# Rotary embedding, one core: tile 3 loaded in one piece, tile 1's store timed by VectorE, tile 2's store on GpSimd's queue

## The chip, the core and the metric

One core of one Trainium2 chip. The metric is the device time of one execution in microseconds. Times below are medians of runs that are all fast; the core's span in the profile is some 1.9 us shorter than the device time. Every batch of runs also timed the kernel before on the same chip, and a ratio is the mean time of a kernel's fast runs over that of the kernel before, so it is not quite the ratio of the medians quoted.

## The reference

`x` is 16 x 512 x 16 x 64 in fp32 (33.55 MB), `cos` and `sin` are 512 x 32. The first half of the last dimension is rotated in quarters and the second half is passed through, so every byte of `x` is read once and written once.

```python
x1, x2 = x[..., :32], x[..., 32:]
first  = x1[..., :16] * cos[..., :16] - x1[..., 16:] * sin[..., :16]
second = x1[..., :16] * sin[..., :16] + x1[..., 16:] * cos[..., :16]
out = concatenate([first, second, x2], axis=-1)
```

## The kernel before

`x` is cut into four tiles of 128 partitions x 64 KB, which pass through a ring of three places in SBUF. VectorE rotates half a tile (8 of 16 rows of 4 KB per partition) with four instructions, in place. Tile 3 takes the place of tile 0, so its load waits for tile 0's store to land.

```python
ring = const_pool.tile([P, NS, K, H, D], fp32)        # NS = 3, K = 16
# load(t, lo, hi) and store(t, lo, hi): one DMA each on nc.sync, rows lo to hi of tile t
load(0)
load(1)
load(2, 0, KC)                                         # KC = 8
# ... cos and sin are loaded on nc.gpsimd and spread into `table` (cut)

def rotate(t, lo, hi):
    # x1, c, s, b_t: views of rows lo to hi (cut)
    nc.vector.tensor_mul(out=b_t, in0=x1, in1=s)
    nc.vector.tensor_mul(out=x1, in0=x1, in1=c)
    nc.vector.tensor_sub(...)                          # cut
    nc.vector.tensor_add(...)                          # cut

def turn(t):
    rotate(t, 0, KC)
    rotate(t, KC, K)
    return store(t)

turn(0)
load(2, KC, K)
near = load(3, 0, KL)                                  # KL = 14
load(3, KL, K)
tc.add_manual_dep(turn(1).ins, near.ins.name, ...)     # tile 1's store waits for `near`
turn(2)
turn(3)
```

## Time and profile before

| | before |
|---|---|
| device time, three runs | 161.51 us (161.4 to 161.61) |
| profiled execution: time, span | 162.1 us, 160.3 us |
| VectorE busy | 112.4 us, its last instruction ends at 130.6 us |
| 16 DMA engines busy with SP's and GpSimd's packets | 97.6% + 0.2% of the span |
| tile 1's store issued, landed | 98.96, 120.72 us |
| tile 3's store issued, landed | 130.6, 159.29 us |

The landing times are the last of the 16 semaphore updates of a DMA in the trace. DVE is VectorE, POOL is GpSimd, SP is SyncE; q1 is the DMA queue that SP fills, q0 that of GpSimd. Below, "row" of a transfer means what one partition of it holds (64 KB of a whole tile), which is one packet of a DMA engine; 16 engines share the 128 partitions, so a tile is 8 rows for each engine. The rows that KC, KL and KM count in the code are others: the 16 pieces of 4 KB in each partition. The profiled execution was a long one (162.1 us). The prediction shows the page, the stretches and SP's waits. The order of the arithmetic and the stores around the changed wait is in the timeline (start and length in us, engine, line, operation; "x3" merges three issues, the first of them at the start shown):

```profile
90.28 4.43 DVE L96 TENSOR_TENSOR b_t<-ring,table 128x4096 f32<-128x4096 f32 x1
94.75 4.42 DVE L97 TENSOR_TENSOR ring<-ring,table 128x4096 f32<-128x4096 f32 x1
98.96 31.98 SPq L58 DMA_DIRECT2D out_dram<-ring  x3
```

Tile 1's store goes out at 98.96, in the middle of tile 2's second half.

### The profile page before, as it was taken

The page shows a single profiled execution, that of the slowest core. Times are in us where ns is not written, and L with a number is a line of the kernel's source. Part 1 is how long each engine was busy: PE and PEld are TensorE (multiplying, and loading weights), DVE is VectorE, ACT ScalarE, POOL GpSimd, SP SyncE. Part 2 cuts the span into 40 slices and gives each one's busy share as a digit, 9 for nine tenths or more (in the row PEclk, how much of TensorE's full clock was granted, in tenths as well). Part 3 has the DMA queues.
Part 4 walks back from the last instruction along what each step waited for, and adds up shares of the span by engine and source line. Part 5 has one row for each costly group of instructions (what it writes and reads, how often), then busy time and mean ns, then how long its engine had stood idle before and what let it go on. Part 6 is the DMA issues. An engine that isn't in the chain of part 4 may idle for free.

```text
span 160.3 us, 113 instructions
## 1 busy us (share of the span) xinstructions
DVE 112.4 (70%) x43; POOL 1.4 (1%) x6
## 2 busy tenths in 40 slices
DVE  1000959999999999999999999999999950000000
POOL 3000000000000000000000000000000000000000
DMA  7969969699699996999999995996996996996990
GB/s 262 540 262 540 491 294 523 278 507 491 294 392 441 474 523 262 523 392 392 499 482 458 458 444 253 546 523 262 523 523 262 523 507 278 523 507 278 523 507 16
DMA packets 1504, 67.24 MB, mean 419 GB/s; under 512 B 192, under 2 KB 192, under 8 KB 224
## 3 DMA queue, kind: packets, MB, share of 16 engines
q1 hardware_dynamic: 1440, 67.11, 97.6%
q0 software_dynamic: 64, 0.13, 0.2%
HBM read 33.69 MB, written 33.55 MB: 419 GB/s over the span
## 4 chain that ended last, share of the span: by engine, by line
DVE 59%; DMA 14%; issue 7%; DVEq 1%
DVE b_t L96 22%; DVE ring L97 22%; DMA ring<-in_x_dram 14%; DVE ring L101 10%; DVE ring L98 4%; DVEq L148 1%; DVEq L96 0%
## 5 line engine op out<-in xcount | busy, mean ns | idle before, releaser
L96 DVE TENSOR_TENSOR b_t<-ring,table 128x4096 f32<-128x4096 f32 x8 | 35.5, 4432 | 2.1 <-DMA ring<-in_x_dram 1.9
L97 DVE TENSOR_TENSOR ring<-ring,table 128x4096 f32<-128x4096 f32 x8 | 35.4, 4424 | 0.3
L98 DVE TENSOR_TENSOR ring<-ring,b_t 128x2048 f32<-128x2048 f32 x8 | 18.3, 2287 | 0.3
L101 DVE TENSOR_TENSOR ring<-ring,b_t 128x2048 f32<-128x2048 f32 x8 | 18.2, 2280 | 0.0
L73 DVE LOAD_MASK_SELECT spun<-stage x1 | 0.0, 14 | 14.4 <-DMA stage<-in_sin_dram 14.4
L83 DVE COPY table<-packed 32x1024 f32<-32x1024 f32 x4 | 2.7, 684 | 0.1
L80 DVE COPY packed<-spun 32x512 f32<-32x512 f32 (+3 forms) x4 | 1.7, 416 | 0.1
L61 DVE MEMSET stage<- 128x512 f32 x1 | 0.5, 485 | 0.9 <-PEq L137 0.9
L73 DVE STREAM_SHUFFLE spun<-stage 128x512 f32<-128x512 f32 x1 | 0.7, 723 | 0.0
L63 POOL DMA_DIRECT2D stage<-in_cos_dram x1 | 0.6, 649 | 1.3 <-DVE stage L61 1.3
L64 POOL DMA_DIRECT2D stage<-in_sin_dram x1 | 0.5, 532 | 0.0
L137 POOL MEMSET const-float32-0.0<- 128x1 f32 x1 | 0.1, 93 | 0.2 <-issue 0.2
L137 POOL MEMSET const-bfloat16-1.0<- 128x1 bf16 x1 | 0.1, 95 | 0.0
L137 POOL MEMSET const-uint8-127<- 128x1 uint8 x1 | 0.1, 93 | 0.0
L137 POOL MEMSET const-float32-1.0<- 128x1 f32 x1 | 0.1, 92 | 0.0
## 6 DMA issues: line engine op xcount, KB each, us to landing
ring<-in_x_dram SPq DMA_DIRECT2D x2, 4096.0 KB, 41.4
ring<-in_x_dram SPq DMA_DIRECT2D x1, 7168.0 KB, 26.4
ring<-in_x_dram SPq DMA_DIRECT2D x1, 1024.0 KB, 28.5
stage<-in_cos_dram POOLq DMA_DIRECT2D x1, 64.0 KB, 9.0
stage<-in_sin_dram POOLq DMA_DIRECT2D x1, 64.0 KB, 13.4
out_dram<-ring SPq DMA_DIRECT2D x4, 25.6
ring<-in_x_dram SPq DMA_DIRECT2D x2, 32.0
```

What stands on the lines that cost most here:

```text
L61: nc.vector.memset(stage[:, :, :, 0:Q], 0.0)
L63: nc.gpsimd.dma_start(out=spread[:, 0, 0], in_=cosf)
L64: nc.gpsimd.dma_start(out=spread[:, 0, 1], in_=sinf)
L73: nc.vector.stream_shuffle(out=spun[:], in_=stage.rearrange("p t k j -> p (t k) j")[:, :, 0:Q], mask=[j % PQ * REP for j in range(PB)],)
L80: nc.vector.tensor_copy(out=packed[0:n], in_=spun[q * PB : q * PB + n])
L83: nc.vector.tensor_copy(out=table[r * PB : (r + 1) * PB].rearrange("p t k c j -> p (t k) c j"), in_=packed.unsqueeze(2).to_broadcast((PB, ...
L96: nc.vector.tensor_mul(out=b_t, in0=x1, in1=s)
L97: nc.vector.tensor_mul(out=x1, in0=x1, in1=c)
L98: nc.vector.tensor_sub(out=x1[:, :, :, 0:Q], in0=x1[:, :, :, 0:Q], in1=b_t[:, :, :, Q:HF])
L101: nc.vector.tensor_add(out=x1[:, :, :, Q:HF], in0=x1[:, :, :, Q:HF], in1=b_t[:, :, :, 0:Q])
L137: nc = _bacc.Bacc("TRN2", target_bir_lowering=False, num_devices=1)
L148: with _tile.TileContext(nc) as tc:
```

## The change

Tile 3 is loaded by one DMA, without the short extra load. Tile 1's store is still held back by an added dependency, but now until VectorE has finished the pieces 8 to 12 of tile 2 (up to KM = 13), and no longer until a load lands. Tile 2's store is issued by GpSimd on its own queue, so that it does not stand in line behind tile 1's.

```diff
--- before.py
+++ after.py
@@ -31,7 +31,7 @@
     R = H * D
     NS = 3
     KC = K // 2
-    KL = 14
+    KM = 13
 
     xf = x.rearrange("b s h d -> (b s h d)").rearrange("(t p f) -> t p f", t=T, p=P)
     of = out.rearrange("b s h d -> (b s h d)").rearrange("(t p f) -> t p f", t=T, p=P)
@@ -54,8 +54,8 @@
     def load(t, lo=0, hi=K):
         return nc.sync.dma_start(out=rows(t, lo, hi), in_=xf[t, :, lo * R : hi * R])
 
-    def store(t, lo=0, hi=K):
-        return nc.sync.dma_start(out=of[t, :, lo * R : hi * R], in_=rows(t, lo, hi))
+    def store(t, lo=0, hi=K, queue=nc.sync):
+        return queue.dma_start(out=of[t, :, lo * R : hi * R], in_=rows(t, lo, hi))
 
 
     nc.vector.memset(stage[:, :, :, 0:Q], 0.0)
@@ -98,28 +98,32 @@
         nc.vector.tensor_sub(
             out=x1[:, :, :, 0:Q], in0=x1[:, :, :, 0:Q], in1=b_t[:, :, :, Q:HF]
         )
-        nc.vector.tensor_add(
+        return nc.vector.tensor_add(
             out=x1[:, :, :, Q:HF], in0=x1[:, :, :, Q:HF], in1=b_t[:, :, :, 0:Q]
         )
 
-    def turn(t):
-        rotate(t, 0, KC)
-        rotate(t, KC, K)
-        return store(t)
-
-    turn(0)
+    rotate(0, 0, KC)
+    rotate(0, KC, K)
+    store(0)
     load(2, KC, K)
-    near = load(3, 0, KL)
-    load(3, KL, K)
+    load(3)
+    rotate(1, 0, KC)
+    rotate(1, KC, K)
+    behind_loads = store(1)
+    rotate(2, 0, KC)
+    near = rotate(2, KC, KM)
+    rotate(2, KM, K)
+    store(2, queue=nc.gpsimd)
 
     tc.add_manual_dep(
-        turn(1).ins,
+        behind_loads.ins,
         near.ins.name,
         mybir.DependencyInfo(mybir.DependencyClass.Sync, mybir.DependencyReason.DATA),
         reason="the store follows the loads at the DMA engines",
     )
-    turn(2)
-    turn(3)
+    rotate(3, 0, KC)
+    rotate(3, KC, K)
+    store(3)
 
 
 # ---- launch: one core; inputs and outputs as the reference has them ----
```

## The prediction

> **What bounds the kernel now.** I read the page first: its slices, its table of DMA queues, then its chain.
>
> ```profile
> span 160.3 us, 113 instructions
> DVE 112.4 (70%) x43; POOL 1.4 (1%) x6
> DMA packets 1504, 67.24 MB, mean 419 GB/s; under 512 B 192, under 2 KB 192, under 8 KB 224
> q1 hardware_dynamic: 1440, 67.11, 97.6%
> q0 software_dynamic: 64, 0.13, 0.2%
> ```
>
> VectorE (DVE) works 70% of the span and does nothing after its last instruction at 130.6 us. The 16 DMA engines are another matter: packets of the SP queue (q1) fill 97.6% of their time and those of GpSimd's queue (q0) 0.2%, together 97.8% of 160.3, or 156.8 us. Only 3.5 us are left, and the next view shows that they lie at the two ends. Its stretches are cut where a transfer ends in the trace's packet records, since packets of 64 KB would otherwise fall on either side of a cut; the columns are DVE busy, GpSimd busy, clock, DMA share and GB/s.
>
> ```profile
> 0.00:1.70 1.70, 0.48 (x1) 0.20 (x4) 1.00 0.00 0
> ...
> 22.10:52.10 30.00, 28.84 (x9) 0.00 (x0) 1.00 1.00 422
> 52.10:71.40 19.30, 19.16 (x6) 0.00 (x0) 1.00 0.99 431
> 71.40:100.50 29.10, 28.86 (x10) 0.00 (x0) 1.00 1.03 446
> 100.50:139.20 38.70, 29.87 (x10) 0.00 (x0) 1.00 1.01 439
> 139.20:158.40 19.20, 0.00 (x0) 0.00 (x0) 1.00 0.94 406
> 158.40:160.30 1.90, 0.00 (x0) 0.00 (x0) 1.00 0.00 0
> ```
>
> Nothing moves for 1.7 us at the start and 1.9 us at the end; between those the share is about 1.00 in every stretch (the 1.03 and 0.94 are packets counted whole on one side of a cut). So the kernel is bound by its transfers: 33.69 MB read and 33.55 MB written, on DMA engines that never pause. The packet records say the same more finely: a row of 64 KB takes 2.418 us on its engine, and its successor starts 2.41 to 2.42 us after it, also across the ends of transfers.
>
> Next, the waits of the SP queue, to see what orders the transfers.
>
> ```profile
> SPq L58 <- DVE ring L101: 57.7, 3, 26.9
> SPq L58 <- DMA ring<-in_x_dram: 46.5, 2, 25.6
> SPq L148 <- DMA out_dram<-ring: 28.3, 1, 28.3
> SPq L55 <- DMA out_dram<-ring: 21.7, 1, 21.7
> ```
>
> The 25.6 us is tile 1's store, ready when DVE finished tile 1 at 76.8 but held until the large part of tile 3's load landed at 98.9. It looks like a big cost, and it is the wait that the change rewrites. But the engines had loads to do in those 25.6 us, and the store's first packets start at 100.46, just where the short part of the load ends. A wait of the issuing queue costs time only if the DMA engines run dry, and here they don't. The chain of waits is of little use here: it follows DVE and stops at 130.6 us, though the last 28 us are stores alone.
>
> **What the Trainium skill says.** "DMA: Bandwidth & Descriptors", section "Issuing engines are not separate DMA queues", says that DMAs from SP, ScalarE and GpSimd end up on the same 16 engines and interleave, and that a second issuer saves only the time to issue. The trace agrees as far as it goes: an issue on SP takes 0.33 to 0.43 us, all of it beside transfers. The same page, "Queues, rings and completion order", says that an engine takes turns between the queues at packet granularity. The trace shows this in small: the 4 KB packets of cos and sin at 7.3 us go between two 64 KB packets without a gap. The section "SWDGE vs HWDGE vs iDMA" says that a packet of the software-made kind is preferably at most 4096 B. The cos and sin packets are 4096 B, but their rows are of 2 KB, so the trace does not tell what becomes of a 64 KB row. "SBUF — State Buffer", section "SBUF: two separate sides", warns that VectorE in a two-port mode locks GpSimd out while it writes descriptors. DVE's work here is tensor_tensor in fp32: 4.43 us for 4096 elements, or 1.08 ns each, so it runs at the plain rate and I do not expect that lock. No store from GpSimd in this trace shows it.
>
> **The change part by part.** Bytes do not change, nor do loads and stores in number of rows per engine: 64 rows of 64 KB each (67.11 MB over 16 engines and 65,536 B).
>
> *Load of tile 3 whole.* In the records a packet of 57,344 B takes 2.116 us, one of 8192 B 0.309. Each engine did 8 of each: 8 x (2.116 + 0.309) = 19.40 us. Now it does 8 x 2.418 = 19.34 us. That removes 0.06 us from the path that sets the end, and one semaphore packet of 0.009 us. Call it 0.07.
>
> *The wait of tile 1's store.* It now waits for the last instruction of rows 8 to 12 of tile 2. DVE starts the second half of tile 2 at 90.28. Its four kinds of instruction take 4.43, 4.42, 2.29 and 2.28 us for 8 rows. The split is about 1.04 ns an element and 0.15 us fixed, so for 5 of 8 rows: 2.83 + 2.82 + 1.49 + 1.48 = 8.62 us, less 0.08 overlap, plus gaps of 0.06. The store is released at about 98.9 us (estimate), where the load released it at 98.96. Load 3 should leave the earliest engines at about 100.4, and the first load took from 0.74 to 1.74 us between issue and first packet, so the store is in the ring just in time, as before. Gain nil; if the release came 0.3 us later, a gap of 0.3 us at most.
>
> *DVE.* Four instructions more, each for its fixed 0.15 us and a gap of 0.02: 0.7 us. DVE ends at 131.3 instead of 130.6. Tile 3's store then joins a queue that, in the before trace, is busy with tile 2's store until 139.1. So 8 us of slack absorb it.
>
> *Tile 2's store on GpSimd's queue.* Issued at about 104.5, it no longer stands behind tile 1's store but takes turns with it. What an engine has to do after 100.5 is 24 rows either way, 24 x 2.418 = 58.0 us, which is 100.4 to 158.4. Who goes first changes landing times, not the sum: the end follows tile 3's store or the remainder of tile 2's, whichever is last. The cost depends on packet size. With whole rows it is nil. Cut into 4 KB packets of 0.159 us (cos and sin rows), a row takes 16 x 0.159 = 2.544 us, and 8 rows 20.35 instead of 19.34: 1.0 us more, all of it on the path.
>
> The sum: -0.07 with whole rows, +0.94 with 4 KB packets. From 161.51 that makes 161.4 or 162.5 us.
>
> **The rivals.** *The early wait paid, and its removal gains.* For it: 25.6 us is the longest wait that touches this store. Against: the new wait ends at the same instant, and the DMA share beside it is full. Even with every gap and every slow packet gone (64 x 2.418 = 154.8 us of packets against 156.8 in the records) there are only 2.0 us to win, and those lie in the first 50 us, which the change does not touch: packets of tiles 0 and 1 took up to 3.3 us. So faster by 2%, 3.2 us, is nearly excluded.
>
> *GpSimd makes descriptors too slowly, and the engines starve.* If rows are cut to 4 KB, GpSimd must make 2048 pieces. Tile 1's store has then almost all the bandwidth until about 121, and tile 2's store alone feeds the engines from there until tile 3's store comes at 131. Against: the issues of cos and sin took 0.65 and 0.53 us for 32 rows, so at most 20 ns a row with the fixed part in it. At 20 ns, 2048 pieces take 41 us from 104.5. By 121 some 800 exist, by 132 some 1400, while engines at 4 KB per 0.159 us on each of 16 would use about 1100 in those 11 us. So no gap, or a small one. At twice that per piece the gap would be 3 to 4 us: 165 us, slower by 2%.
>
> *The mixture of two stores is slower than one.* The hardware queue's loads and stores ran at 2.418 us a row alike; nothing in the trace mixes two large transfers from two queues, so I can't exclude some per cent on 27 us of overlap. One per cent would be 0.3 us.
>
> **Range and chances.** I give whole rows 65%, 4 KB packets or another small cost of the second queue 30%, and starvation 5%. The middle lies near the first case, a little above: 161.6 us. The three runs of before span only 0.2 us, so the low end needs little room, 161.1; the high end takes in the 4 KB case, 162.7. Faster 1%, within 2% 96%, slower 3%.
>
> **What the profile of the changed kernel would show.** Packets of q0: 64 + 128 and their semaphores if rows stay whole, some 2100 if they are cut, with hundreds or thousands more in the page's count and the share of 16 engines' span up by about 0.6%. The DMA share should be full from 1.7 us to the end of the last store; tile 1's store issued between 98.7 and 99.2; DVE's end at 131.3; tile 1's store landing later than 120.7 if the two stores share evenly, near 121 if q0's packets are small. The prediction is wrong if the share drops below 0.95 anywhere between 100 and 158 us, if packets of 64 KB on q1 take clearly more than 2.418 us beside q0's, or if DVE's instructions after 104 us are longer than before.

## The result and the profile after

161.51 us (161.4 to 161.64, six runs) against 161.5 us (161.4 to 161.7, six runs): a ratio of 0.9999, 95% interval 0.9986 to 1.0012. The change does nothing to the time. The page's lines that answer to those of before:

```profile
span 159.5 us, 115 instructions
...
DVE 112.9 (71%) x47; POOL 1.9 (1%) x7
...
DMA packets 1360, 67.24 MB, mean 422 GB/s; under 512 B 176, under 2 KB 176, under 8 KB 208
...
q1 hardware_dynamic: 1152, 58.72, 85.7%
q0 software_dynamic: 208, 8.52, 12.4%
```

Tile 2's 8.39 MB have moved from q1 to q0. Of the 208 packets of q0, 32 are those of cos and sin, 48 are semaphore updates (three DMAs x 16 engines), which leaves 128: GpSimd's store kept its rows of 64 KB whole. Together the queues fill 98.1% of the span, against 97.8%. The stretches, cut at the ends of rows (DVE busy, GpSimd busy, clock, DMA share, GB/s):

```profile
22.00:51.00 29.00, 27.80 (x9) 0.00 (x0) 1.00 1.00 434
51.00:71.00 20.00, 19.86 (x6) 0.00 (x0) 1.00 1.02 434
71.00:99.80 28.80, 28.52 (x12) 0.00 (x0) 1.00 0.99 427
99.80:109.50 9.70, 9.56 (x6) 0.56 (x1) 1.00 1.00 432
109.50:131.20 21.70, 21.53 (x7) 0.00 (x0) 1.00 1.00 435
131.20:143.40 12.20, 0.00 (x0) 0.00 (x0) 1.00 0.99 430
143.40:157.90 14.50, 0.00 (x0) 0.00 (x0) 1.00 1.00 434
```

The DMA engines are as full as before. The page's span is 0.8 us shorter than that of before, but this is no gain: the unprofiled spans are 159.5 to 159.6 here and, in the later batches, 159.6 to 160.0 for the kernel before with one of 160.8, and the profiled execution of before had slow rows where nothing was changed (422 GB/s from 22.1 to 52.1 us, against 434 here). SP's waits and the timeline:

```profile
SPq L58 <- DVE ring L101: 84.1, 3, 30.5
...
SPq L58 <- DMA ring<-in_x_dram: 22.3, 2, 20.8
SPq L55 <- DMA out_dram<-ring: 21.0, 1, 21.0
```

```profile
97.35 1.48 DVE L101 TENSOR_TENSOR ring<-ring,b_t 128x1280 f32<-128x1280 f32 x1
98.86 32.68 SPq L58 DMA_DIRECT2D out_dram<-ring  x2
98.86 1.77 DVE L96 TENSOR_TENSOR b_t<-ring,table 128x1536 f32<-128x1536 f32 x1
...
104.31 4.43 DVE L96 TENSOR_TENSOR b_t<-ring,table 128x4096 f32<-128x4096 f32 x1
104.58 0.56 POOL L58 DMA_DIRECT2D out_dram<-ring  x1 [101.70 <-DVE ring L101]
```

The wait of 25.6 us for the load is gone, and one on VectorE has taken its place: tile 1's store goes out at 98.86 instead of 98.96. That is the same instant, 0.1 us apart. GpSimd's store goes out at 104.58, and the trace shows its rows from 109.52 on in strict turns with those of SP's queue, one of q0, one of q1, each 2.42 us, until the last row of tile 1's store ends at 129.2; then three rows of q0 follow each other, and the turns start again at 136.16 with tile 3's store. So tile 1's store lands at 132.05 instead of 120.72, tile 2's at 144.11 instead of 140.01, and the last at 158.58 instead of 159.29. The 24 rows per engine of the three last stores take 58.09 us on the earliest engine (99.85 to 157.94) and took 57.95 before (100.46 to 158.41): the sum is kept, the order is not.

### The profile page after: what moved, and what is told of

Read it like the earlier page. It is cut to its first block, busy times and chain, and to the rows that moved or that the text cites. A ratio compares the mean times of both kernels' runs of the same rounds, so it can differ in the third digit from the quotient of the medians.

```text
span 159.5 us, 115 instructions
## 1 busy us (share of the span) xinstructions
DVE 112.9 (71%) x47; POOL 1.9 (1%) x7
## 4 chain that ended last, share of the span: by engine, by line
DVE 61%; DMA 14%; issue 5%; DVEq 1%
DVE b_t L96 22%; DVE ring L97 22%; DMA ring<-in_x_dram 14%; DVE ring L101 10%; DVE ring L98 7%; DVEq L152 1%; DVEq L96 0%
## 5 line engine op out<-in xcount | busy, mean ns | idle before, releaser
L96 DVE TENSOR_TENSOR b_t<-ring,table 128x4096 f32<-128x4096 f32 (+2 forms) x9 | 35.6, 3959 | 2.1 <-DMA ring<-in_x_dram 1.9
L97 DVE TENSOR_TENSOR ring<-ring,table 128x4096 f32<-128x4096 f32 (+2 forms) x9 | 35.6, 3950 | 0.3
L98 DVE TENSOR_TENSOR ring<-ring,b_t 128x2048 f32<-128x2048 f32 (+2 forms) x9 | 18.4, 2050 | 0.3
L101 DVE TENSOR_TENSOR ring<-ring,b_t 128x2048 f32<-128x2048 f32 (+2 forms) x9 | 18.4, 2043 | 0.0
L58 POOL DMA_DIRECT2D out_dram<-ring x1 | 0.6, 559 | 101.7 <-DVE ring L101 101.7
```

Source lines behind the costliest of these rows:

```text
L58: return queue.dma_start(out=of[t, :, lo * R : hi * R], in_=rows(t, lo, hi))
L98: nc.vector.tensor_sub(out=x1[:, :, :, 0:Q], in0=x1[:, :, :, 0:Q], in1=b_t[:, :, :, Q:HF])
L101: return nc.vector.tensor_add(out=x1[:, :, :, Q:HF], in0=x1[:, :, :, Q:HF], in1=b_t[:, :, :, 0:Q])
```

## The experiments

First theory, the prediction's: the DMA engines are full, so queue and order don't matter and a wait costs only what time the engines stand dry. Rivals: two effects that cancel; a wait that does something although the engines are full; VectorE's chain as the bound.

### Tile 2's store back on SP's queue

```diff
-    store(2, queue=nc.gpsimd)
+    store(2)
```

> The changed kernel with tile 2's store back on SP's queue. Theory (the 16 DMA engines are full from 1.7 us on, so an issuer changes only who goes first): 161.4 to 161.6 us, as both kernels; tile 1's store lands near 120.5 instead of 132.05, tile 2's near 139.5 instead of 144.1, the last at 158.5 as before. In the mixed stretch of the changed kernel 24 rows per engine took 58.09 us against 57.95 in the kernel before, so at most 0.15 us is won back. Rival (two queues cost something that the whole load of tile 3 paid for, so that two effects cancel): 0.3 us or more faster than both.

161.77 us (161.52 to 161.83), ratio to the kernel before 1.0013 (1.0001 to 1.0025). Tile 1's store landed at 120.17, tile 2's at 139.47, the last at 158.78. The time is slightly above what was expected, and not below as the rival wants. From the landing of load 3 to the end this kernel took 158.78 - 100.88 = 57.90 us, the changed one 158.58 - 100.69 = 57.89. So GpSimd's queue neither costs nor gains. In the profiled executions the 0.2 us arose before 100 us, where the two programs are the same instruction for instruction: the rows that started from 67 to 75 us took 0.67 us too long per engine, against 0.38 in the changed kernel. I take it for a difference between chips or executions and have no run that shows which.

### The added wait taken out

```diff
-    tc.add_manual_dep(
-        behind_loads.ins,
-        near.ins.name,
-        ...
-    )
```

> The changed kernel with the added dependency of tile 1's store taken out (no data needs it), so that it is issued when VectorE has finished tile 1, near 76.8 us, behind tile 3's load on the same queue. Theory: the engines of a queue take rows in the order of issue, load 3 lands at 100.7 as before, time 161.4 to 161.6. Rival 1 (a store close behind a load disturbs it, which is what the wait was for): load 3 lands later than 102 or its rows take over 2.45 us, and the time rises by 1 us or more. Rival 2 (the wait held the kernel back): faster by 1 us or more.

162.87 us (162.56 to 162.9), ratio 1.008 (1.0068 to 1.0092): 1.4 us slower than the changed kernel's median. The first theory is wrong here, and rival 1 is right: the wait is worth more than a microsecond although no engine stands dry with it or without it. The store is issued at 76.84, and the place is visible in two stretches, first of the changed kernel, then of this one. The stretch 94.5 to 98.5 holds the start of exactly the last two rows of load 3 on each engine:

```profile
94.50:98.50 4.00, 3.97 (x3) 0.00 (x0) 1.00 1.21 524
```

```profile
94.50:98.50 4.00, 3.97 (x3) 0.00 (x0) 1.00 1.46 524
```

A packet is counted whole in the stretch in which it starts, so a share can exceed 1. The bytes are the same (524 GB/s), but the packets took 1.46 instead of 1.21 of the stretch: 0.25 x 4.0 = 1.0 us more on each engine. In the packet records it is the last row alone: 3.01 to 3.85 us, median 3.36, where the row before it and all store rows after it took 2.418. Everything after comes that much later: load 3 lands at 101.74 (100.69), the last store at 159.75 (158.58).

### Neither wait nor GpSimd's queue

```diff
-    store(2, queue=nc.gpsimd)
+    store(2)
-    tc.add_manual_dep(...)          # as in the run above
```

> The changed kernel with no added dependency and every store on SP's queue; load 3 stays whole. Theory: 161.4 to 161.6 us, so that neither kernel's arrangement does anything. If waits or queues each cost something that the other hides, this one differs from both by 0.3 us or more.

162.80 us (162.39 to 163.09), ratio 1.0078. It agrees with the run above within the spread: the cost belongs to the missing wait, on one queue or two. This kernel's profile is a poor witness: it is of its fastest execution (162.39), with the last row of load 3 at a median of 2.63 us, and 0.73 us per engine of its loss lie in slow rows between 20 and 47 us, as in the profile of the kernel before (0.78). So the cost at the last row is not the same in every execution.

### No arithmetic

```diff
-    rotate(0, 0, KC)
-    rotate(0, KC, K)
     ...                             # all rotations and the added wait out, transfers as they were
```

> The changed kernel's transfers without any rotation (a wrong result on purpose: the output is x); the added dependency goes with the arithmetic it hung on. Theory: nothing of VectorE's 107 us lies on the path that sets the end, so 161.3 to 161.6 us. Rival (the end is set by VectorE's chain at 131 us plus a last store, as the chain of waits suggests): many us faster.

162.71 us (162.19 to 163.25). Its output is wrong, which doesn't matter for the time. Without 107 us of VectorE's work the kernel is not faster, so VectorE's chain does not set the end. It is 1.2 us slower, which I had not expected. The trace points to the same cost at another place: with nothing to wait for, tile 0's store is issued at 22.98 instead of 49.87 and stands behind the loads of tile 1 and of tile 2's first half. The last two rows of 32 KB of tile 2's load before that store then took 1.87 and 1.69 us in the median (up to 2.14), where 1.213 is normal, 1.09 us more per engine; and here too the rows after the change of direction are normal:

```profile
47.50:52.30 4.80, 0.00 (x0) 0.00 (x0) 1.00 1.10 375
52.30:62.00 9.70, 0.00 (x0) 0.00 (x0) 1.00 1.03 446
```

A full share at 375 GB/s, then 446. In the other kernels VectorE releases tile 0's store at about 50 us, when the rows before it are nearly through. From 88 to 112 us this kernel also takes turns between load rows (q1) and store rows (q0); after one slower load row at the start of that (median 2.58), all took 2.418 but for single ones. So a change of direction between two queues does not cost each time.

### The point moved later

```diff
-    KM = 13
+    KM = 15
```

> The changed kernel with the point in tile 2's arithmetic moved two rows on (13 to 15): tile 1's store released near 102.1 instead of 98.86. Load 3's rows leave the engines from 99.85 to 100.26, and an issue took about 1.0 us to its first packet at the start, so the engines stand idle from about 100 to 103.1. Theory: a wait costs exactly the time for which the engines run dry: 3.0 to 3.4 us, 164.5 to 165.0 us. Rival (the wait's point doesn't matter, because tile 2's store or the slack at VectorE makes up for it): 161.5.

```diff
-    near = rotate(2, KC, KM)
-    rotate(2, KM, K)
+    rotate(2, KC, KM)
+    near = rotate(2, KM, K)
```

> The changed kernel with tile 1's store waiting for the end of tile 2's arithmetic, near 104.3 instead of 98.86; GpSimd's store is issued at the same time. Theory: engines idle from about 100.1 to 105.3, 5.0 to 5.4 us: 166.5 to 167.0 us, with a loss that is 2.2 us over that of the point at 15 rows, the further delay. Rival: 161.5, or a loss well under the delay.

164.72 us (164.28 to 164.85; ratio 1.0192) and 166.99 us (166.77 to 167.11; ratio 1.0336). Here the engines do stand dry, in the first and in the second kernel:

```profile
95.00:100.20 5.20, 5.17 (x3) 0.00 (x0) 1.00 0.93 403
100.20:103.00 2.80, 2.73 (x4) 0.00 (x0) 1.00 0.00 0
103.00:112.50 9.50, 9.40 (x5) 0.56 (x1) 1.00 1.03 442
```

```profile
95.00:100.20 5.20, 5.13 (x4) 0.00 (x0) 1.00 0.93 403
100.20:105.20 5.00, 4.90 (x5) 0.49 (x1) 1.00 0.00 0
105.20:115.00 9.80, 9.73 (x3) 0.07 (x1) 1.00 1.00 428
```

The stores go out at 102.24 and 104.44. Load 3's last rows end from about 99.95 to 100.4, the first store rows start at 103.08 and 105.29: some 3.0 and 5.2 us dry, against 3.2 and 5.5 us lost. The difference of the two, 2.3 us, is the 2.2 us between the issues. On this side the prediction's rule holds.

### The point moved earlier

```diff
-    KM = 13
+    KM = 11
```

> The changed kernel with the point moved two rows earlier (13 to 11), so that tile 1's store is released near 95.65, some 1.8 us before the last row of load 3 starts on the engines (97.43 to 97.84 in the changed kernel). The first theory (order alone counts) is already wrong by 1.3 us without the wait. Second theory: what costs is that a store stands in the queue when the last load row starts, however long it has stood there; then this costs as much as no wait, 162.5 to 163.0 us, with that row at 3.0 us or more in the trace. Rival: the cost grows with the time for which store and load are queued together; then most of it is gone, 161.5 to 161.9.

```diff
-    KM = 13
+    KM = 12
```

> The changed kernel with the point one row earlier (12): the store is released near 97.26, just before the last load row starts, and about 1.0 to 1.5 us later its rows can be fetched, so in the middle of that row. Second theory: the store comes after that row has started, so 161.4 to 161.7 us; rival (it must come after the row has nearly ended): 162.0 to 163.0.

162.66 us (162.47 to 162.91; ratio 1.006, 1.0038 to 1.0081) and 161.88 us (161.64 to 162.17; ratio 1.0017, 0.9993 to 1.0041). In one and the other, for the same two rows as above:

```profile
94.50:98.50 4.00, 3.93 (x4) 0.00 (x0) 1.00 1.47 524
```

```profile
94.50:98.50 4.00, 3.93 (x4) 0.00 (x0) 1.00 1.27 524
```

With the point two pieces earlier the store goes out at 95.57, 1.9 us before the last load row starts, and the whole cost is there: that row took 3.33 us in the median, as with a store that had stood in the queue since 76.84. With one piece earlier the store goes out at 97.24, as that row starts, and a part is left in the trace (2.67 us in the median, up to 3.00): 0.25 us per engine. Its median time is a little more than the second theory allowed, but the ratio's interval includes 1, so the time alone does not show this part. All six points together:

| tile 1's store issued | last row of load 3, median | engines dry | time |
|---|---|---|---|
| 76.84 (no wait) | 3.36 us | none | 162.87 us |
| 95.57 | 3.33 us | none | 162.66 us |
| 97.24 | 2.67 us | none | 161.88 us |
| 98.86 (the changed kernel) | 2.42 us | none | 161.51 us |
| 102.24 | 2.42 us | 3.0 us | 164.72 us |
| 104.44 | 2.42 us | 5.2 us | 166.99 us |

So the cost does not grow with the time the store stands in the queue; what counts, with these 64 KB rows, is whether it stands there when the last load row starts. The valley lies between 95.57 and 102.24, where the time has clearly risen on either side, and the changed kernel lies in it.

### The kernel before, without its wait

```diff
-    tc.add_manual_dep(
-        turn(1).ins,
-        near.ins.name,
-        ...
-    )
+    turn(1)
```

> The kernel before with its own wait taken out: tile 1's store is issued when VectorE has finished tile 1, near 76.8, instead of at 98.96. Second theory (a store that stands in the queue while the load's last rows start costs 1.0 to 1.3 us, and both kernels' waits avoid that to the same degree): 162.4 to 163.0 us, as the changed kernel without its wait. Rival (the short last load of 8 KB rows already protects the kernel before, and its wait is idle): 161.4 to 161.7.

162.65 us (162.23 to 162.95), ratio 1.0066 (1.005 to 1.0082). The old wait did the same work as the new one: without it the 8 KB packets of the short load took 0.4125 us in the mean instead of 0.3096, 0.8 us over the 8 packets of each engine. The first is this kernel, the second the kernel before:

```profile
97.80:100.60 2.80, 2.77 (x2) 0.00 (x0) 1.00 0.98 293
```

```profile
97.80:100.60 2.80, 2.77 (x2) 0.00 (x0) 1.00 1.43 609
```

(Fewer bytes start in the first stretch at a full share; the 1.43 is that of store rows which begin just before 100.6.) So the short load alone is no protection. Nor is it one packet alone that slows: the first 8 KB packet of each engine kept 0.310 us in the mean, the other seven took 0.427. With rows of 64 KB it was the last one, without arithmetic the last two of 32 KB, here seven of eight of 8 KB: in all three it is about the last 64 KB that an engine loads, and 0.8 to 1.1 us more.

### Both suspected costs of small packets, made on purpose

```diff
-    store(2, queue=nc.gpsimd)
+    for k in range(K):
+        store(2, k, k + 1, queue=nc.gpsimd)
```

> The changed kernel with tile 2's store cut into 16 stores of one 4 KB row per partition on GpSimd's queue: the case of small packets that the prediction feared, made on purpose. Packets of 4 KB took 0.159 us, so 8 x (16 x 0.159 - 2.418) = 1.0 us more on every engine and 16 semaphore packets of 0.009: 162.5 to 162.7 us if the engines stay full. If GpSimd's issues (0.56 us each, with waits for earlier landings between them) leave the engines dry between tile 1's store and tile 3's: 163.5 to 168.

163.87 us (163.6 to 164.26), ratio 1.0146: 2.4 us more, above the first range and inside the second, but not for the reason given there. The 2048 packets of 4 KB took 0.159 us each, so the 1.0 us for packet size and 0.14 for semaphores are there. No stretch between the stores is dry: GpSimd's waits for earlier pieces, 24.1 us in all, lie beside full engines. The rest looks like the cost found above. The first half's pieces need only the first half of tile 2 and went out from 90.50 on, while load 3 was still coming, and its last rows took 3.34 us in the median and up to 3.7, although SP's store went out at 98.87 as in the changed kernel; so a store on the other queue seems able to do it too; this one trace does not separate it from the small pieces themselves. It is 0.93 us more per engine between 90 and 100 us (whole rows at 2.418 us make 434 GB/s at a full share; 0.84 of that would be 364):

```profile
97.00:101.50 4.50, 4.43 (x4) 0.00 (x0) 1.00 0.84 276
101.50:106.00 4.50, 4.43 (x4) 0.53 (x1) 1.00 1.43 612
```

1.0 + 0.14 + 0.93 = 2.1 of the 2.4 us.

```diff
-    load(3)
+    for k in range(K):
+        load(3, k, k + 1)
```

> The changed kernel with tile 3's load cut into 16 loads of one 4 KB row per partition on SP's queue: the cost of cutting that load, made larger. In the kernel before, cutting off 2 of 16 rows as a load of its own added 0.06 us to each engine's packets; here 8 x (16 x 0.159 - 2.418) + 16 x 0.009 = 1.15 us, so 162.5 to 162.8 us. If SP's waits between the pieces let the engines run dry: more than 163.5. If a cut load costs nothing: 161.5.

163.09 us (162.91 to 163.23), ratio 1.0096: 1.6 us more, above the range by 0.3. The packets took 0.1623 us in the mean and not 0.159, so an engine's 128 need 20.77 us where 8 whole rows need 19.34: 1.43, and with 0.14 for 15 more semaphore packets 1.57. The engines stayed full. The longer packets are spread from 88 us on and are not the cost found above: the store was issued at 98.99, 2.3 to 2.6 us before the load's last piece ended on each engine, and the pieces after that kept 0.163 us. So a load cut to 4 KB pieces does cost, and the cut of before (two of 16 rows, as packets of 8 KB) is small by comparison, as predicted; its 0.06 us is too small for these runs to show.

### The same for a load behind a store

```diff
+    tc.add_manual_dep(
+        behind_store.ins,            # the load of tile 2's second half
+        early.ins.name,              # the first multiplication of tile 1's second half
+        ...
+    )
```

> The changed kernel, and in addition the second half of tile 2's load waits for the first multiplication of tile 1's second half, near 67.8 us, instead of standing behind tile 0's store from 50.3. In the changed kernel's trace the last row of that store, started at 67.9 to 68.5, takes up to 3.3 us, 0.38 us more per engine than 2.418. If a load queued behind a store costs as a store queued behind a load does, this wait takes that away: 161.0 to 161.3 us, better than both kernels. Rival (that row is slow by chance or for another reason; the kernel before showed none there): 161.5. If the load comes too late, a gap near 70.5 and more than 161.8.

161.57 us (161.38 to 162.21), ratio 0.9998 (0.9976 to 1.0019). No gain. The load went out at 67.83 instead of 50.3, and the rows around 70 us together took 0.35 us too long per engine, against 0.38 in the changed kernel; they are only others: the first rows of the load more, the last of the store less. The comparison is weak, since this sum varies between executions: in ten other traces with a load standing behind this store and rows of normal length before the store it is 0.35 to 0.67 us; in those of the kernel before, of the run with neither wait nor GpSimd's queue and of the run without arithmetic it is 0, after 0.8 to 1.1 us of slow rows between 20 and 53 us. So a load behind a store is not cured by timing it like this; whether another instant would do it is open. None of the runs gave a version that beats both kernels.

## Why the prediction was right, and where it was not

**Bound by the DMA engines: right.** The share stays at 0.99 to 1.02 in each stretch shown, and taking out all of the arithmetic made nothing faster. But "a row of 64 KB takes 2.418 us" was too tidy a reading: the rows of tile 1 in that trace took up to 2.71 us, and the prediction's own line shows it as 422 GB/s at a full share of 1.00.

**Tile 2's store at no cost with whole rows: right.** The 65% case came true: 128 packets of 65,536 B. Turns between two queues cost nothing that a run shows (57.89 against 57.90 us after load 3). The 4 KB case was sized rightly: 0.159 us a packet when forced. The rivals of starvation and of a costly mixture are excluded for these transfers: the rows stayed whole, and with 2048 pieces made on purpose the engines stayed full too.

**The load in one piece, -0.07: consistent, not shown.** It is under the spread of 0.2 us.

**VectorE: right.** Release 98.86 (98.9 predicted), end at 131.2 (131.3), and the slack absorbed it. The lock of GpSimd by VectorE is not seen: GpSimd's first row came 4.9 us after its issue beside VectorE's work, and no sooner without any, 5.7 us in the run without arithmetic (82.81 to 88.48). The prediction's reason for not expecting it, VectorE's 1.08 ns an element, was not tested.

**The wait: right in what it makes of this change, wrong as a rule.** The prediction said of the rewritten wait that "A wait of the issuing queue costs time only if the DMA engines run dry": it asked what the wait might cost and not what it might save. (Of the 25.6 us of that wait, the store was ready for about the last 22, from 76.8 to 98.96.) For the time of this change that was enough, since the old and the new wait end 0.1 us apart. That instant was worked out; that an earlier one costs too was not foreseen, and that the rule's gap did no harm here is luck. But the rule is half of the story: a store that stands behind a load when its last row starts makes this row 0.9 us slower in the median, and dropping the wait costs 1.1 us in the kernel before and 1.4 in the changed one. The prediction also called this wait's other risk "a gap of 0.3 us at most" for a release 0.3 us later, and for that side the slope of one for one is shown. The change therefore moved a kernel from one point of the valley to another at the same depth: that is why it is worth nothing, and had the point been set at 11 or 15 pieces, it would have lost 1.1 or 3.2 us.

**What stays open.** Why the last load row slows is not settled. The trace gives starts and lengths of packets and no reason. It is not the change of direction as such, since the turns of load and store rows in the run without arithmetic ran at 2.418 us; but those are turns between two queues, and within one queue no run separates the two. Open too is why the cost was only 0.2 us in the profiled execution of the run with neither wait nor GpSimd's queue, where the store had stood since 76.84. Not explained either are the slow rows before 50 us in single executions and the 0.2 us of the first experiment.

## What to carry to other kernels

When the DMA engines are full from end to end, moving a transfer to another queue only changes who lands first; look at the sum of rows per engine before expecting time from it. A full share is not yet full speed: compare share and GB/s of the same packets, since a queue order can lengthen single packets while nothing looks idle. A wait that looks useless may hold a store back until just before the load ahead of it ends; before removing or re-anchoring one, find out what its instant protects, and move it in both directions to see how wide the valley is.

## What the Trainium skill lacked or had wrong

- "DMA: Bandwidth & Descriptors", "Queues, rings and completion order": it says nothing of what a store does that stands behind a load. Here the load's last row of 64 KB took 3.36 us (median; up to 3.85) with a store behind it and 2.418 with the store issued 1.0 to 1.4 us before the row's end; 1.1 to 1.4 us of the kernel's time.
- The same page, "SWDGE vs HWDGE vs iDMA", gives a packet as preferably at most 4096 B. A store of 64 KB rows from GpSimd's queue moved as 128 packets of 65,536 B, 2.42 us each, so for this store the preference did not bind.
- The same page, "Queues, rings and completion order", says that an engine takes turns at packet granularity; with 64 KB packets the turn is 2.42 us. It does not say how long a newcomer waits for its first turn beside the other queue's rows: here it took 4.9 us on GpSimd's queue (104.58 to 109.52; 4.5 to 6.1 in the other runs) and 5.0 us on SP's (tile 3's store, 131.19 to 136.16), while SP's store issued onto dry engines began after 0.84 us (102.24 to 103.08).
